# Convolution taps ordered behind each chain of queries or keys, and both ranges of rotated keys split in one operation per engine

## The chip, the core and the metric

The kernel runs on one core of one Trainium2 chip. The time is device microseconds of one execution; the kernel before takes 1058.18 us, the median of 3 runs. In this text TensorE is PE in the rows of the profile, VectorE is DVE, ScalarE is ACT, GpSimd is POOL and SyncE is SP.

## The reference

The network has two layers over 256 latent tokens (4 rows of 64 columns) and 256 context tokens, 1024 wide, in float32. Each layer has a token-mixing and a channel-mixing stage. The edited code belongs to the first of them: one input projection gives the columns of a convolution branch, of queries, keys and values of 8 heads, and of two gates.

```python
h = modulate(rmsnorm(x, norm1_g[l]), sh1, sc1)
p = h @ w_in[l]
q, k, v = (split_heads(u) for u in jnp.split(p[..., GLU_END:QKV_END], 3, axis=-1))
q = rope_2d(q, pos_row, pos_col)
k = rope_2d(k, pos_row, pos_col)
y_conv = conv_branch(p[..., :GLU_END], conv_dw[l], conv_dw_b[l], conv_ln_g[l],
                     conv_ln_b[l], w_conv_out[l])
y_attn = merge_heads(neighbourhood_attention(q, k, v, k_c, v_c, na_rpb[l])) @ w_na_out[l]
x = x + g1 * gated_merge(p[..., QKV_END:], y_conv, y_attn, w_out[l])
```

A latent query sees the keys of 16 columns in all 4 rows, with a bias, and all 256 context keys, in one softmax. In layer 0 the context tokens run through the same stage with an attention of their own; in layer 1, the last, they only give keys and values. The convolution branch is a gated linear unit, 31 taps along the tokens for each of its 512 channels, a LayerNorm, a silu and a projection.

## The kernel before

**Matmuls.** Tokens are columns, channels are partitions. A float32 product is made of three matmuls with reduced operands: every weight and every activation is kept as a high part and a remainder, and `mm3` (L197, L198, L199) adds high times high, remainder times high and high times remainder in PSUM. SyncE loads a block of weights (`raw`, 512 KB, four buffers), ACT rounds it to the high part (`whi`, L167 or L216), and the remainder comes from DVE (`wlo`, L168) or from ACT (L217) with an accumulating DMA of GpSimd (L218). Layer 0 works on 512 columns (latent and context tokens), layer 1 on 256, its keys on 512.

**PSUM.** There are 4 banks `main` for groups of the projection, and `sc` (2), `pt` and `po` for attention. A group has 24 matmuls per block of 128 channels. It can start only when the DVE and ACT operations that read its bank before have ended.

**Queries and keys.** `qk(j)` runs for the four pairs of heads j = 0 to 3. For queries and then for keys it calls `in_group` and sends DVE and ACT through a chain: product with the cosines (L859), swap of the halves (L860), product with the sines (L861), and their sum (L864 for queries, which also reorders columns into blocks; L869 for keys). Then high part and remainder of each piece of the result: ACT writes the high part (L881), DVE the remainder (L882). For keys the pieces are the context keys (`qk<-main`, 256 elements, read from PSUM) and two ranges of rotated columns, the last 40 of each row and the first 40 (`qk<-t`, 4 rows x 40, that is 160 elements). These are stored column by column, so that the four rows of a column lie side by side; neighbours of a row stand 16 bytes apart. For queries there is one latent piece of 256, and in layer 0 one of 256 for the context.

**Attention.** `att.pair` (on L884) queues the pair. Steps of attention are issued between groups of the projection: `products` (L495, TensorE), `scores` (bias and maximum on DVE, L516; exponential on ACT, L519; reciprocal on DVE, L521; scaling on ACT, L522), `turn` (transposes on TensorE, L561, and their copies on ACT, L564 or L567) and `values` (L578, L587; L595 and L596 take the result).

**Taps.** The convolution is 31 taps in each of 4 blocks, 124 in a layer: `tap` (L671 for the first of a block, L673 for the others), a multiply-add of a whole block on DVE. They wait in a list and are issued a few at a time by slots inside the groups of the projection (`rate`, 2 or 3 per slot). `conv_tap` issues a tap with an order behind the operation in `after[0]`: a tap that is issued later may not come ahead of it on DVE. Before, `after[0]` is set only by scores, latent (L516) and context (L530); the scheduler is free to put taps between the operations of a chain. A layer's taps end in `ss` (L949 to L951), the sum for the LayerNorm, for which TensorE waits at L955.

The order on each engine is fixed when the kernel is built; engines wait for one another through semaphores.

Of the kernel before, what the change touches and what calls it, by code (L numbers as in the profile page):

```python
# [8 lines left out]
F32 = mybir.dt.float32  # L9
# [3 lines left out]
ALU = mybir.AluOpType  # L13
# [7 lines left out]
GW = 64  # L21
# [11 lines left out]
LAT, CTX = slice(0, S), slice(S, 2 * S)  # L33
ROWS = S // GW
NB_, BC = 4, 16
WC, TC = 32, 40
BASE = (0, 8, 24, 32)
KL, KX, KN = ROWS * TC, ROWS * TC + S, 2 * ROWS * TC + S
# [15 lines left out]
def trunk(ctx: ExitStack, tc: tile.TileContext, xt, cvec, crow, wall, wada, params, bias_t, rope_t, out):  # L54
# [368 lines left out]
    class Attention:  # L423
# [147 lines left out]
        def values(self, what, js, pT, bank):  # L571
# [19 lines left out]
            for n, j in enumerate(js):  # L591
# [3 lines left out]
                act.copy(to[0], src)  # L595
                dve.tensor_tensor(to[1], src, to[0].bitcast(F32), ALU.subtract)  # L596

    def blocks(ap):
        return ap.rearrange("p (r b c) -> p b r c", r=ROWS, b=NB_)

# [31 lines left out]
    for l in range(DEPTH):  # L632
# [5 lines left out]
        with ExitStack() if last else start as e1a:  # L638
# [74 lines left out]
            with ExitStack() as e1b:  # L713
# [129 lines left out]
                def qk(j):  # L843
# [4 lines left out]
                    for what in range(2):  # L848
                        w = T if what == 0 else 2 * S
                        sc = HD ** -0.5 if what == 0 else 1.0  # L850
                        ps = in_group((T_Q, T_K)[what] + j, slice(0, w))
                        if what == 0:
                            with tc.issue_after(lastdma[0].ins):
                                sp.dma_start(bt, bias_t[l, j])
                        r1, r2 = tmp(), tmp()
                        got = back(ps[:, :w])
                        lat, ctx_ = (got[:, 0], got[:, 1]) if w > S else (got, None)
                        part = halves if w == S else lambda a: a
                        dve.tensor_tensor(part(r1[:, LAT]), lat, part(rope[:, 0, :]), ALU.mult)  # L859
                        dve.stream_shuffle(part(r2[:, LAT]), lat, SWAP16)  # L860
                        dve.tensor_tensor(r2[:, LAT], r2[:, LAT], rope[:, 1, :], ALU.mult)  # L861
                        if what == 0:
                            rq = tmp()
                            dve.tensor_tensor(  # L864
                                rq[:, LAT].rearrange("p (b r c) -> p b r c", b=NB_, r=ROWS),
                                blocks(r1[:, LAT]), blocks(r2[:, LAT]), ALU.add,
                            )
                        else:
                            dve.tensor_tensor(r1[:, LAT], r1[:, LAT], r2[:, LAT], ALU.add)  # L869
                        f = eb.tile([P, 2, KN if what else w], F32R, tag="qk"[what], bufs=2, name=nm("qk"))  # L870
                        if what == 0:
                            to = [([f[:, a, LAT] for a in range(2)], rq[:, LAT])]
                            if T > S:
                                to.append(([f[:, a, CTX] for a in range(2)], ctx_))
                        else:
                            rv_ = r1[:, LAT].rearrange("p (r c) -> p r c", r=ROWS)
                            to = [([f[:, a, KCTX] for a in range(2)], ctx_)]
                            for d, c in ((slice(0, KL), slice(GW - TC, GW)), (slice(KX, KN), slice(0, TC))):
                                to.append(([f[:, a, d].rearrange("p (c r) -> p r c", r=ROWS) for a in range(2)], rv_[:, :, c]))
                        for (hi, lo), src in to:  # L880
                            act.activation(hi, src, AF.Identity, scale=sc)  # L881
                            end = dve.scalar_tensor_tensor(lo, src, sc, hi.bitcast(F32), ALU.mult, ALU.subtract)  # L882
                        both.append(f)
                    att.pair(j, *both, bt, end)  # L884

# [471 lines left out]
```

## Time and profile before

| | |
|---|---|
| median of 3 runs | 1058.18 us |
| lowest and highest | 1057.49 and 1059.27 us |
| the profiled execution | 1054.58 us, its span 1052.8 us |
| mean granted clock of TensorE | 0.997 |
| instructions | 17991 |
| HBM read | 187.63 MB, 179 GB/s over the span with what is written |

The profiled execution is one of its own, 3.6 us below the median. The profile names an instruction by engine, line of the kernel, operation and tiles, output first (`qk<-t`); a duration runs from the start to the end of one instruction, and since neighbours overlap on an engine, two of them can start closer together than either lasts. Layer 0's token mixing takes from about 58 to 240 us, its channel mixing to about 685, layer 1's token mixing to about 840, and its channel mixing the rest.

### The profile page before, as it was taken

What the parts mean: (1) busy time and instruction counts of PE and PEld (TensorE: products, weight loads), DVE (VectorE), ACT (ScalarE), POOL (GpSimd) and SP (SyncE); (2) the same over time, 40 slices, a digit from 0 to 9 for tenths busy, and PEclk for the clock granted to TensorE, in tenths of its full rate; (3) what the DMA queues carried; (4) which work ended last, traced back from release to release, by engine and by line L of the source; (5) the groups of instructions that cost most, each with busy time, mean ns of one, the idle gap of its engine ahead of it and who ended that gap; (6) DMA issues with size and microseconds to landing.
All of it is one profiled execution on the core that took longest, in us unless ns stands there. A gap on an engine that the chain in (4) does not pass through costs nothing.

```text
span 1052.8 us, 17991 instructions
## 1 busy us (share of the span) xinstructions
PE 1032.4 (98%) x6886; PEld 932.9 (89%) x6886; DVE 893.2 (85%) x1608; ACT 565.6 (54%) x921; POOL 43.7 (4%) x59
## 2 busy tenths in 40 slices
PE   9999999999999999999999999999999999999997
PEld 7787788888889988888888889999889999999996
DVE  6568899999998787878788888799899988988883
ACT  4458768545434644444444223545777666766652
POOL 1111110011000000000000000000000000000000
PEclk9999999999999999999999999999999999999998
DMA  9989674888945345454545887556734485666781
GB/s 374 305 221 229 156 181 121 258 255 236 305 146 177 104 140 160 140 164 143 166 145 160 301 289 249 180 189 209 208 123 135 161 292 176 193 201 199 221 283 57
DMA packets 59511, 209.26 MB, mean 199 GB/s; under 512 B 7201, under 2 KB 7457, under 8 KB 59425
## 3 DMA queue, kind: packets, MB, share of 16 engines
q1 hardware_dynamic: 54384, 190.77, 55.3%
q0 software_dynamic: 4752, 17.30, 8.7%
q8 instruction: 54, 0.88, 0.3%
q14 instruction: 33, 0.26, 0.1%
q10 hardware_dynamic: 288, 0.04, 0.0%
HBM read 187.63 MB, written 1.05 MB: 179 GB/s over the span
## 4 chain that ended last, share of the span: by engine, by line
PE 68%; DVE 17%; ACT 5%; DMA 4%; issue 3%; SPq 1%; DVEq 0%; ACTq 0%
PE main L197 20%; PE main L198 20%; PE main L199 20%; DVE cb L673 6%; PE main L736 4%; DVE wlo L168 3%; DMA raw<-in_wall 2%; DVE t L304 2%; DMA own<-in_wada 1%; SPq L728 1%; PE sc L197 1%; PE sc L199 1%; PE sc L198 1%; DVE qk L882 1%; ACT pp L519 1%
## 5 line engine op out<-in xcount | busy, mean ns | idle before, releaser
L197 PE MATMUL main<-h,whi 128*128 128x256 f32 (+1 forms) x1328 | 433.1, 326 | 1.2 <-DVE qk L882 1.2
L198 PE MATMUL main<-h,whi 128*128 128x256 f32 (+1 forms) x1328 | 430.2, 324 | 0.9 <-DVE h L1001 0.7
L199 PE MATMUL main<-h,wlo 128*128 128x256 f32 (+1 forms) x1328 | 429.9, 324 | 1.2 <-DVE wlo L168 1.1
L167 ACT CAST whi<-raw 128x1024 fp32r<-128x1024 f32 (+1 forms) x211 | 218.3, 1039 | 234.8 <-PE main L198 173.6
L168 DVE TENSOR_TENSOR wlo<-raw,whi 128x1024 fp32r<-128x1024 f32 (+1 forms) x211 | 253.6, 1208 | 67.2 <-ACT whi L167 66.4
L197 PEld LDWEIGHTS main<-h,whi 128*128 128x128 f32 x1328 | 252.8, 190 | 22.0 <-issue 1.3
L199 PEld LDWEIGHTS main<-h,wlo 128*128 128x128 f32 x1328 | 252.5, 190 | 18.5 <-DVE wlo L168 1.8
L198 PEld LDWEIGHTS main<-h,whi 128*128 128x128 f32 x1328 | 252.7, 190 | 18.3 <-DVE h L1001 1.0
L304 DVE CUSTOM_DVE_ANT_0 t<-own,sb,par 128x1024 bf16<-128x1024 f32 x120 | 151.8, 1282 | 6.8 <-DMA own<-in_wada 6.8
L673 DVE SCALAR_TENSOR_TENSOR cb<-u,par,cb 128x512 f32<-128x512 f32 (+1 forms) x240 | 144.7, 620 | 2.8
L198 PE MATMUL main<-fl,whi 128*128 128x256 f32 (+1 forms) x396 | 122.8, 310 | 0.0
L197 PE MATMUL main<-fh,whi 128*128 128x256 f32 (+1 forms) x396 | 122.8, 310 | 0.0
L199 PE MATMUL main<-fh,wlo 128*128 128x256 f32 (+1 forms) x396 | 122.5, 310 | 0.0
L197 PEld LDWEIGHTS main<-fh,whi 128*128 128x128 f32 x396 | 75.6, 191 | 3.8 <-ACT fh L1095 0.2
L198 PEld LDWEIGHTS main<-fl,whi 128*128 128x128 f32 x396 | 75.6, 191 | 3.7 <-DVE fl L1096 0.2
L199 PEld LDWEIGHTS main<-fh,wlo 128*128 128x128 f32 x396 | 75.5, 191 | 3.6
L216 ACT CAST whi<-raw 128x1024 fp32r<-128x1024 f32 x33 | 34.6, 1049 | 36.0 <-PE main L198 30.5
L404 ACT ACTIVATE h<-t,mod 128x256 fp32r<-128x256 f32 x56 | 25.2, 503 | 34.8 <-DVE t L403 34.3
L218 POOL DMA_DIRECT2D wlo<-raw x33 | 28.9, 877 | 258.9 <-ACT wlo L217 107.6
L736 PE MATMUL main<-whi,h 128*128 128x512 f32 x128 | 38.5, 386 | 0.2
L1105 ACT ACTIVATE t<-t 128x512 f32<-128x512 f32 x22 | 13.9, 632 | 41.3 <-DVE t L1074 41.3
L217 ACT ACTIVATE wlo<-whi 128x1024 fp32r<-128x1024 f32 x33 | 35.0, 1061 | 0.5
(214 smaller groups left out, 1268.8 us busy)
## 6 DMA issues: line engine op xcount, KB each, us to landing
raw<-in_wall SPq DMA_DIRECT2D x240, 512.0 KB, 4.3
own<-in_wada SPq DMA_DIRECT2D x72, 512.0 KB, 4.7
wlo<-raw POOLq DMA_DIRECT2D x33, 512.0 KB, 5.4
raw<-in_wada SPq DMA_DIRECT2D x16, 512.0 KB, 5.8
bias<-in_bias_t SPq DMA_DIRECT2D x8, 520.0 KB, 5.3
row<-in_wada SPq DMA_DIRECT2D x8, 512.0 KB, 5.1
sb<-in_crow SPq DMA_DIRECT2D x5, 512.0 KB, 4.8
x<-in_xt SPq DMA_DIRECT2D x4, 512.0 KB, 5.1
```

What stands on the lines that cost most here:

```text
L167: act.copy(hi[:, c], r[:, c])
L168: dve.tensor_tensor(lo[:, c], r[:, c], hi[:, c].bitcast(F32), ALU.subtract)
L197: pe.matmul(ps, w[0], order(xh), start=start, stop=False)
L198: pe.matmul(ps, w[0], order(xl), start=False, stop=False)
L199: pe.matmul(ps, w[1], order(xh), start=False, stop=stop)
L216: act.copy(hi, r)
L217: act.mul(lo, hi.bitcast(F32), -1.0)
L218: pool.dma_start(lo, r, accum_op=ALU.add)
L304: dve.tensor_tensor_reduce(tmp().bitcast(BF16), r, v, 1.0, pr(l, BADA + n, 1), ALU.mult, ALU.add, mods[l][:, n, s : s + 1])
L404: high = act.activation(hi[:, c], y[:, c], AF.Identity, bias=b)
L673: dve.scalar_tensor_tensor(cb[j], src, w, cb[j], ALU.mult, ALU.add)
L736: mm = pe.matmul(pv[t], h1[n == 1][k][:, c], runs(w[n == 2][:, b]), start=k + n == 0, stop=k == KD - 1 and n == 2)
```

## The change

Two things are changed in `qk(j)`. First, the loop over the two ranges of keys is gone: a helper `steps` builds one access pattern over both ranges, and one ACT copy and one DVE subtraction of 2 x 4 x 40 = 320 elements take the place of two and two. Second, `after[0] = end` is set behind the chain of queries and behind that of keys, so that taps issued from then on are ordered behind its last operation on DVE (L888 for keys, L883 for queries), as they are behind scores.

```diff
@@ -594,6 +594,10 @@
                 src = po[:, c].rearrange("p (b r c) -> p b r c", b=NB_, r=ROWS) if what == LAT else po[:, c]
                 act.copy(to[0], src)
                 dve.tensor_tensor(to[1], src, to[0].bitcast(F32), ALU.subtract)
+
+    def steps(a, first, *dims):
+
+        return bass.AP(tensor=a.tensor, offset=a.offset + first, ap=[a.ap[0], *dims])
 
     def blocks(ap):
         return ap.rearrange("p (r b c) -> p b r c", r=ROWS, b=NB_)
@@ -873,13 +877,16 @@
                             if T > S:
                                 to.append(([f[:, a, CTX] for a in range(2)], ctx_))
                         else:
-                            rv_ = r1[:, LAT].rearrange("p (r c) -> p r c", r=ROWS)
                             to = [([f[:, a, KCTX] for a in range(2)], ctx_)]
-                            for d, c in ((slice(0, KL), slice(GW - TC, GW)), (slice(KX, KN), slice(0, TC))):
-                                to.append(([f[:, a, d].rearrange("p (c r) -> p r c", r=ROWS) for a in range(2)], rv_[:, :, c]))
                         for (hi, lo), src in to:
                             act.activation(hi, src, AF.Identity, scale=sc)
                             end = dve.scalar_tensor_tensor(lo, src, sc, hi.bitcast(F32), ALU.mult, ALU.subtract)
+                        if what:
+                            hi, lo = (steps(f[:, a], 0, (KX, 2), (1, ROWS), (ROWS, TC)) for a in range(2))
+                            src = steps(r1, GW - TC, (TC - GW, 2), (GW, ROWS), (1, TC))
+                            act.copy(hi, src)
+                            end = dve.tensor_tensor(lo, src, hi.bitcast(F32), ALU.subtract)
+                        after[0] = end
                         both.append(f)
                     att.pair(j, *both, bt, end)
```

The lines behind the helper are numbered 4 higher in the changed kernel, and by 6 or 7 more behind the edit: L859, L860, L861, L864 and L869 become L863, L864, L865, L868 and L873, L881 and L882 become L882 and L883, L887 and L888 are new, L671 and L673 become L675 and L677, and the gate's L711 becomes L715. TensorE's and GpSimd's rows stay in their order; on SyncE the load of a bias and one of weights change places. DVE and ACT have 8 instructions fewer each.

DVE in layer 0, the chain of keys of pair 1 (`main_943`, TensorE's group) up to the first scores of the same pair (`sc`). Before:

```order
L859 TENSOR_TENSOR t_1012<-main_943,rope_196 128x256
L860 STREAM_SHUFFLE t_1013<-main_943 128x256
L673 SCALAR_TENSOR_TENSOR cb_0_184<-u_0_197,par,cb_0_184 128x512
L861 TENSOR_TENSOR t_1013<-t_1013,rope_196 128x256
L882 SCALAR_TENSOR_TENSOR qk_1018<-main_943,qk_1018 128x256
L869 TENSOR_TENSOR t_1012<-t_1012,t_1013 128x256
L673 SCALAR_TENSOR_TENSOR cb_0_184<-u_0_197,par,cb_0_184 128x512 x2
L882 SCALAR_TENSOR_TENSOR qk_1018<-t_1012,qk_1018 128x4x40 x2
L673 SCALAR_TENSOR_TENSOR cb_0_184<-u_0_197,par,cb_0_184 128x512 x3
L516 ISA sc_1063,mx_1079<-sc_1063,bias_893 128x2x208
```

With the change, from the same group (now `main_941`):

```order
L863 TENSOR_TENSOR t_1010<-main_941,rope_196 128x256
L677 SCALAR_TENSOR_TENSOR cb_0_184<-u_0_197,par,cb_0_184 128x512
L864 STREAM_SHUFFLE t_1011<-main_941 128x256
L865 TENSOR_TENSOR t_1011<-t_1011,rope_196 128x256
L873 TENSOR_TENSOR t_1010<-t_1010,t_1011 128x256
L883 SCALAR_TENSOR_TENSOR qk_1016<-main_941,qk_1016 128x256
L888 TENSOR_TENSOR qk_1016<-t_1010,qk_1016 128x2x4x40
L677 SCALAR_TENSOR_TENSOR cb_0_184<-u_0_197,par,cb_0_184 128x512 x5
L516 ISA sc_1059,mx_1075<-sc_1059,bias_891 128x2x208
L516 ISA mx_1075 128x1
L677 SCALAR_TENSOR_TENSOR cb_0_184<-u_0_197,par,cb_0_184 128x512
```

The taps that stood between L869 and L882 have moved behind L888, and one of them stands between the two scores.

DVE in layer 1, behind the last scores of pair 0 (`L516` on `main_7303` and `main_7293`, just ahead of these rows), with the end of the chain of keys of pair 1 (`qk_7348`, `qk_7338`) and the start of the chain of queries of pair 2 (`main_7392`, `main_7380`). Before:

```order
L673 SCALAR_TENSOR_TENSOR cb_1_6567<-u_1_6580,par,cb_1_6567 128x256
L671 TENSOR_SCALAR cb_2_6568<-u_2_6581,par 128x256
L673 SCALAR_TENSOR_TENSOR cb_1_6567<-u_1_6580,par,cb_1_6567 128x256
L521 RECIPROCAL ri_7331<-sm_7329 128x1
L673 SCALAR_TENSOR_TENSOR cb_2_6568<-u_2_6581,par,cb_2_6568 128x256
L673 SCALAR_TENSOR_TENSOR cb_1_6567<-u_1_6580,par,cb_1_6567 128x256
L521 RECIPROCAL ri_7339<-sm_7337 128x1
L673 SCALAR_TENSOR_TENSOR cb_2_6568<-u_2_6581,par,cb_2_6568 128x256
L882 SCALAR_TENSOR_TENSOR qk_7348<-t_7342,qk_7348 128x4x40
L673 SCALAR_TENSOR_TENSOR cb_1_6567<-u_1_6580,par,cb_1_6567 128x256
L859 TENSOR_TENSOR t_7428<-main_7392,rope_6578 128x256
L882 SCALAR_TENSOR_TENSOR qk_7348<-t_7342,qk_7348 128x4x40
```

With the change:

```order
L521 RECIPROCAL ri_7321<-sm_7319 128x1
L521 RECIPROCAL ri_7329<-sm_7327 128x1
L863 TENSOR_TENSOR t_7416<-main_7380,rope_6570 128x256
L864 STREAM_SHUFFLE t_7417<-main_7380 128x256
L888 TENSOR_TENSOR qk_7338<-t_7332,qk_7338 128x2x4x40
L677 SCALAR_TENSOR_TENSOR cb_1_6559<-u_1_6572,par,cb_1_6559 128x256
L675 TENSOR_SCALAR cb_2_6560<-u_2_6573,par 128x256
L677 SCALAR_TENSOR_TENSOR cb_1_6559<-u_1_6572,par,cb_1_6559 128x256
L865 TENSOR_TENSOR t_7417<-t_7417,rope_6570 128x256
L677 SCALAR_TENSOR_TENSOR cb_1_6559<-u_1_6572,par,cb_1_6559 128x256
L868 TENSOR_TENSOR t_7421<-t_7416,t_7417 128x256
```

The taps that stood around the two reciprocals and between the two L882 now stand behind L888, and L888 behind both reciprocals and the first two operations on the next queries.

ACT at the same place. Before:

```order
L519 ACTIVATE pp_7336,sm_7337<-main_7303,mx_7334 128x416
L522 ACTIVATE pp_7328<-pp_7328,ri_7331 128x416
L881 ACTIVATE qk_7348<-t_7342 128x4x40
L522 ACTIVATE pp_7336<-pp_7336,ri_7339 128x416
L881 ACTIVATE qk_7348<-t_7342 128x4x40
L711 ACTIVATE g_1_7389<-main_7355 128x256
```

With the change:

```order
L519 ACTIVATE pp_7326,sm_7327<-main_7293,mx_7324 128x416
L522 ACTIVATE pp_7318<-pp_7318,ri_7321 128x416
L522 ACTIVATE pp_7326<-pp_7326,ri_7329 128x416
L887 CAST qk_7338<-t_7332 128x2x4x40
L715 ACTIVATE g_1_7377<-main_7343 128x256
```

The high parts of the two ranges stood on either side of the last L522; the one L887 stands behind it.

ACT in layer 1 one pair later, at the end of the exponentials of pair 1 (`pp_7550` and `pp_7538`) with the high parts of the keys of pair 2 (`qk_7562`, `qk_7550`). Before:

```order
L519 ACTIVATE pp_7542,sm_7543<-pt_7516,mx_7540 128x416
L519 ACTIVATE pp_7550,sm_7551<-main_7517,mx_7548 128x416
L522 ACTIVATE pp_7542<-pp_7542,ri_7545 128x416
L522 ACTIVATE pp_7550<-pp_7550,ri_7553 128x416
L881 ACTIVATE qk_7562<-t_7556 128x4x40 x2
L711 ACTIVATE g_2_7604<-main_7569 128x256
L167 CAST whi_7836<-raw_7835 128x1024
```

With the change:

```order
L522 ACTIVATE pp_7522<-pp_7522,ri_7525 128x416
L522 ACTIVATE pp_7530<-pp_7530,ri_7533 128x416
L519 ACTIVATE pp_7538,sm_7539<-main_7505,mx_7536 128x416
L882 ACTIVATE qk_7550<-main_7426 128x256
L715 ACTIVATE g_2_7590<-main_7555 128x256
L522 ACTIVATE pp_7538<-pp_7538,ri_7541 128x416
L167 CAST whi_7820<-raw_7819 128x1024
L887 CAST qk_7550<-t_7544 128x2x4x40
```

The high part of the context keys (`qk<-main`), which stood ahead of all exponentials of this softmax, now stands behind the last of them, and that of the ranges behind one more L522 and a weight cast (L167).

## The prediction

> **What bounds the kernel now.** I read the page's busy shares first, then the table of stretches, then what TensorE waits for, then the groups by shape, and last the timeline around single chains.
>
> ```profile
> PE 1032.4 (98%) x6886; PEld 932.9 (89%) x6886; DVE 893.2 (85%) x1608; ACT 565.6 (54%) x921; POOL 43.7 (4%) x59
> ...
> 105.00:145.00 40.00, 37.99 (x258) 32.29 (x257) 35.98 (x78) 30.18 (x66) 5.21 (x6) 1.00 0.66 160
> 740.00:800.00 60.00, 58.63 (x555) 52.77 (x554) 57.07 (x148) 47.63 (x103) 3.17 (x3) 1.00 0.51 154
> 800.00:840.00 40.00, 38.83 (x352) 37.82 (x350) 38.00 (x85) 24.34 (x48) 0.71 (x1) 1.00 0.51 159
> ```
>
> After the length of a stretch stand the busy times of PE, PEld, DVE, ACT and POOL, then the granted clock. TensorE is busy for 98% of the span, so another order on DVE can win no more than the gaps it leaves TensorE. The edited code runs from 58 us on (layer 0) and around 740 to 800 us (layer 1). In layer 1 DVE is nearly full as well: 57.07 of 60 us, then 38.00 of 40. A hole made in its row there is not easily filled later. The clock is 1.00 in all three, so it is no term. What TensorE waits for over the whole span (total us, times, longest):
>
> ```profile
> PE pt L370 <- DVE ss L356: 2.0, 3, 1.0
> ...
> PE sc L495 <- ACT pT L567: 1.7, 1, 1.7
> PE main L197 <- DVE qk L882: 1.2, 2, 0.6
> ...
> PE po L955 <- DVE ss L951: 1.0, 1, 1.0
> PE sc L495 <- ACT qk L881: 0.9, 1, 0.9
> ...
> PE sc L495 <- DVE qk L882: 0.6, 1, 0.6
> ```
>
> Two things are to be seen. The waits that earlier chains can end (L881, L882, and L567, whose copies stand behind chain operations on ACT) add up to 0.9 + 1.2 + 0.6 + 1.7 = 4.4 us, 0.4% of the time: about the ceiling of the gain. And each stage ends in a wait on DVE itself: layer 0 in `ss L951` (1.0 us), layer 1 in `ss L356` (1.0 us the longest). Behind such a wait only DVE's own finishing time counts, and what TensorE gained earlier is lost there unless DVE comes earlier too. **So I make the sum on DVE's time, layer by layer.**
>
> **The merge.** Per chain of keys two operations of 160 elements become one of 320, on ACT and on DVE; eight chains in all, so 8 instructions fewer on each engine.
>
> ```profile
> L881 ACT ACTIVATE qk<-t 128x160 fp32r<-128x160 f32 x8 | 4.4, 620 | 1.1 <-DVE t L869 1.1
> L882 DVE SCALAR_TENSOR_TENSOR qk<-t,qk 128x160 fp32r<-128x160 f32 x8 | 4.3, 561 | 0.3
> L521 DVE RECIPROCAL ri<-sm 128x1 f32<-128x1 f32 x16 | 2.6, 160 | 1.5 <-ACT pp L519 1.5
> ...
> L882 DVE SCALAR_TENSOR_TENSOR qk<-t,qk 128x256 fp32r<-128x256 f32 x4 | 1.7, 423 | 0.5 <-ACT qk L881 0.5
> ```
>
> 160 elements take 561 ns in layer 1, more than the 423 ns of 256 that lie side by side. No row has the 320-element form. Durations overlap, so I count from start to start: the pair below at 763.90 gives way to a tap at 764.83, 0.93 us for 320 elements; the pair at 96.20 in layer 0 gives way at 96.91, 0.71 us. Bounds for the merged operation are 0.4 us (somewhat over the 256-element form, as L869, 256 elements, gives way to a tap 0.33 us after its start, from 94.41 to 94.74 below) and 0.93 (nothing saved). I take 0.65, nearest to the layer 0 pair less one start: 0.06 us saved per chain in layer 0, 0.28 in layer 1; on ACT I take 0.5 to 0.65. If the bounds held instead, the eight chains would differ by about 1 us to either side; I keep that for the range.
>
> [...]
>
> **Layer 0: later taps, earlier chains.** DVE, TensorE and ACT around the keys of pair 1 (its scores at 99.16) and the context softmax behind pair 2 (start, duration, operation, idle time before it; between them the group of DVE's first score operations in layer 0, with its idle time):
>
> ```profile
> 94.41 0.42 DVE L869 TENSOR_TENSOR t<-t,t 128x256 f32<-128x256 f32 x1
> 94.74 1.54 DVE L673 SCALAR_TENSOR_TENSOR cb<-u,par,cb 128x512 f32<-128x512 f32 x2
> 96.20 0.81 DVE L882 SCALAR_TENSOR_TENSOR qk<-t,qk 128x160 fp32r<-128x160 f32 x2
> 96.91 2.33 DVE L673 SCALAR_TENSOR_TENSOR cb<-u,par,cb 128x512 f32<-128x512 f32 x3
> 99.16 0.59 DVE L516 CUSTOM_DVE_ANT_0 sc<-sc,bias 128x416 f32<-128x416 f32 x1
> ...
> 96.04 0.44 PE L495 MATMUL sc<-qk,qk 64*128 64x416 f32 x2 [0.87 <-ACT qk L881]
> 97.07 0.62 PE L495 MATMUL sc<-qk,qk 64*128 64x416 f32 x4 [0.58 <-DVE qk L882]
> ...
> L516 DVE CUSTOM_DVE_ANT_0 sc<-sc,bias 128x416 f32<-128x416 f32 x4 | 2.4, 592 | 3.3 <-PE sc L495 3.3
> ...
> 125.32 0.81 ACT L881 ACTIVATE qk<-t 128x160 fp32r<-128x160 f32 x2 [1.58 <-DVE t L869]
> 127.98 1.05 ACT L567 COPY pT<-sc 128x512 f32<-128x512 f32 x2
> ...
> 128.60 1.11 PE L495 MATMUL sc<-qk,qk 64*128 64x416 f32 x5 [1.69 <-ACT pT L567]
> ```
>
> The two taps between L869 and L882 (1.46 us from 94.74 to 96.20) now stand behind L888. L888 must then wait for ACT's L887, some 0.45 us, so pair 1's chain ends about 1 us earlier, and TensorE gets back 1.0 to 1.2 of its 0.87 + 0.58. The scores, however, have the same taps ahead of them as before, one more even ahead of the second L516: five, a score, a sixth, a score. With the holes of about 0.65 us in the chain of queries and 0.45 at L888, where taps ran before, the softmax comes 0.7 to 1.1 us later, and the transposes take back what the products won. For pair 2 one tap fewer stands ahead and ACT's two operations become one, so L567, for which TensorE waits at 128.60, comes some 0.8 us earlier (0.73 of a tap and 0.1). On DVE's time: holes +1.1, merges 4 × −0.06, and of the 3.3 us that DVE waits for products in front of the scores about 1.2 (0.8 for pair 2, half of that for the others): **−0.4 us at `ss L951`** (1.1 − 0.24 − 1.2). The ends are −2.4 (1.2 + 0.8 + 0.4 kept) and +1.1 (holes only).
>
> **Layer 1, pair 1: a hole behind the scores.** From here taps may not start before L888, and both reciprocals, L863, L864 and L888 stand ahead of them. The softmax of the pair before, as it ran:
>
> ```profile
> 746.08 0.14 DVE L516 DVE_READ_ACCUMULATOR2_ANT mx<- 128x1 f32 x1
> 746.08 0.48 DVE L673 SCALAR_TENSOR_TENSOR cb<-u,par,cb 128x256 f32<-128x256 f32 x1
> ...
> 746.86 0.20 ACT L519 ACTIVATION_READ_ACCUMULATOR pp<-pt,mx 128x1 f32 x1
> 747.44 0.21 ACT L519 ACTIVATION_READ_ACCUMULATOR pp<-main,mx 128x1 f32 x1
> 747.53 0.65 ACT L522 ACTIVATE pp<-pp,ri 128x416 f32<-128x416 f32 x1
> 748.07 0.64 ACT L881 ACTIVATE qk<-t 128x160 fp32r<-128x160 f32 x1
> 748.39 0.66 ACT L522 ACTIVATE pp<-pp,ri 128x416 f32<-128x416 f32 x1
> ...
> 753.85 0.82 PE L495 MATMUL sc<-qk,qk 64*128 64x416 f32 x3 [0.19 <-ACT pT L564]
> ```
>
> DVE is free at 746.22 (746.08 + 0.14). Before, taps started at once. Now the first reciprocal waits for ACT until 747.06, the second until 747.65; L863 and L864 (0.33 each) then run to 748.45. ACT does both L522 from 747.53, 0.54 apart, so its L887 starts at about 748.6 and lets L888 start at about 749.25. In those 3.03 us DVE works 0.2 (two reciprocals, less than their 160 ns each from start to start) + 0.67, so **2.2 us stand empty** where taps and one of the two L881 and L882 ran. Next to the hole the chain of queries of pair 2 comes 0.7 us earlier, which ends the wait for L564 that TensorE has at 753.85.
>
> **Layer 1, pair 2: the bank and a second hole.**
>
> ```profile
> 761.09 0.42 DVE L882 SCALAR_TENSOR_TENSOR qk<-main,qk 128x256 fp32r<-128x256 f32 x1
> ...
> 761.65 0.45 PE L197 MATMUL main<-h,whi 128*128 128x512 f32 x1 [0.55 <-DVE qk L882]
> ...
> 762.20 1.18 ACT L522 ACTIVATE pp<-pp,ri 128x416 f32<-128x416 f32 x2
> 763.27 1.04 ACT L881 ACTIVATE qk<-t 128x160 fp32r<-128x160 f32 x2
> 763.90 1.04 DVE L882 SCALAR_TENSOR_TENSOR qk<-t,qk 128x160 fp32r<-128x160 f32 x2
> 764.83 0.46 DVE L673 SCALAR_TENSOR_TENSOR cb<-u,par,cb 128x256 f32<-128x256 f32 x1
> ```
>
> TensorE's next group waited for L882 to free its bank. Its successor L883 now needs an ACT copy that stands behind the last exponential, and itself stands behind that exponential's reciprocal and a weight split. ACT is done with the last exponential at about 762.2, as before; the copy takes it to 762.55, DVE's reciprocal and L865 meanwhile to 762.65, L883 to 763.0, where L882 ended at 761.5: that group starts 1.5 us later. ACT then has the gate (0.45), one L522 (0.54), a weight cast (1.0) and L887 (0.6), to about 765.15, while DVE has L873, L863 and L864, 1.0 us from 763.0 on. Before L888 another **1.2 us stand empty**. Pair 3 has a split as cover and loses some 0.15. In sum 2.2 + 1.2 + 0.15 − 3 × 0.28 = **+2.7 us on DVE**. It has to reach `L356`:
>
> ```profile
> 821.51 0.42 DVE L356 TENSOR_TENSOR ss<-ss,t 128x256 f32<-128x256 f32 x1
> ```
>
> TensorE already waited 1.0 us for this row, and DVE has 38.00 busy of the 40 us around it, so nothing ahead of it takes up 2.7. The ends are −0.5 (ACT early enough, 0.28 saved three times) and +3.8 (holes, nothing saved). Queues past which something moves: SyncE swaps one bias load with one weight load, cost nothing while weights have the 0.51 DMA share above; GpSimd's and TensorE's rows stay as they were.
>
> **The sum**: −0.4 + 2.7 = +2.3 us. On the profiled execution's 1054.58 that is 1056.9; the median of the runs is 1058.18, 3.6 above it, and I predict **1060.5** there.
>
> **Rivals.**
> - *Chains win* (faster): the gains stay in both layers and the holes are refilled. For it: the 4.4 us of waits are real. Against it: both stages end in DVE waits. It gives −1.2 − 0.8 − 0.4 in layer 0 and −0.2 − 1.2 (both bank waits) in layer 1: −3.8, 1054.4. Chance 0.20.
> - *Covered* (no change): the order moves, but DVE's holes replace waits it has anyway, and gains and losses cancel. TensorE's row order is unchanged, which speaks for it; 57.07 of 60 us speaks against. 1058.2. Chance 0.17.
> - *Holes in both layers* (slower): the holes in layer 0, +1.1, also reach `ss L951` with nothing shortened, and layer 1 loses 3.2 (the 3.55 of its holes with under half of the merge's gain). It decides as soon as L888 waits in both layers for an ACT copy that stands behind another's work. 1058.2 + 4.3 = 1062.5. Chance 0.13.
>
> **How the numbers follow.** My forecast has the remaining 0.50, with a range of its own from 1058.8 to 1062.0 (layer 1's hole by ±1.0, the merge by ±0.5). A measurement of this kernel tells 0.2%, 2.1 us, from no change; the forecast lies at that edge and gives about half to each side. Faster: 0.20. Same: 0.17 + 0.23 = 0.40. Slower: 0.13 + 0.27 = 0.40. The range 1055.0 to 1062.4 leaves out about half of the faster rival and half of the slowest, under 2 in 10.
>
> **What would show it.** Right: in layer 1, DVE idle time of about 2 us in front of two reciprocals and L888 in pair 1, about 1 us in pair 2; a longer TensorE wait for L883; `L356` about 2.5 us later against the start of the stage, with a wait of over 1 us still on it; in layer 0 the waits at L495 for L887 and L888 mostly gone, with the wait at L561 for L522 grown. Wrong: no wait left on `L951` or `L356`, or an L888 of 0.4 us.

## The result, and the profile after

The changed kernel takes **1063.93 us** (median of 6 runs, 1061.42 to 1065.77) against 1057.84 (6 runs, 1055.06 to 1059.76): a ratio of **1.0057, 95% interval 1.0037 to 1.0077**. It is slower by 6.1 us, where the forecast said 2.3 and the range ended at 1062.4. The profiled execution took 1062.81 us, its span is 1061.0 (before 1052.8).

The stretches of the changed kernel and what its TensorE waits for, in the columns used before:

```profile
58.00:105.00 47.00, 45.15 (x231) 37.94 (x230) 38.74 (x84) 30.86 (x52) 7.14 (x9) 0.96 0.89 224
105.00:145.00 40.00, 36.94 (x262) 30.70 (x261) 34.98 (x74) 30.15 (x68) 4.35 (x5) 0.96 0.56 149
...
740.00:800.00 60.00, 55.69 (x490) 50.01 (x490) 55.42 (x146) 40.92 (x86) 4.72 (x4) 1.00 0.51 157
```

```profile
PE sc L495 <- ACT pT L567: 2.1, 1, 2.1
PE main L197 <- ACT pp L519: 2.0, 1, 2.0
...
PE pt L370 <- DVE ss L356: 1.8, 3, 1.0
PE main L197 <- DVE qk L883: 1.6, 1, 1.6
PE sc L495 <- ACT qk L887: 1.5, 1, 1.5
PE po L578 <- DVE ol L596: 1.4, 1, 1.4
...
PE sc L495 <- DVE qk L888: 0.4, 1, 0.4
...
PE po L962 <- DVE ss L958: 0.3, 1, 0.3
```

None of the waits that the earlier chains could end has gone: L567 has 2.1 us (before 1.7), the first scores 1.5 + 0.4 (before 0.9 + 0.6), and the bank waits have grown from 1.2 to 2.0 + 1.6. The granted clock, 1.00 before, is 0.96 in two stretches.

Where the loss arises is seen by setting TensorE's rows of both profiles side by side, since their order is the same. Against before, TensorE is late by

| at (time in before) | changed | changed again | order only | order, layer 0 | order, layer 1 | merge only |
|---|---|---|---|---|---|---|
| 213 us, end of layer 0's taps | +4.07 | +4.88 | +2.56 | +3.10 | +1.48 | +4.09 |
| 742 us, ahead of layer 1's pair 1 | +4.15 | +5.73 | +3.15 | +4.33 | +3.50 | +5.45 |
| 821 us, end of layer 1's taps | +8.31 | +10.44 | +8.12 | +4.32 | +8.13 | +5.82 |
| **from 742 to 821** | **+4.16** | **+4.71** | **+4.97** | −0.01 | **+4.63** | +0.37 |

The other columns belong to kernels of the next section. Layer 1 is clear: 4.2 to 5.0 us with the new order, next to nothing without. Layer 0 is not: "order, layer 1" runs layer 0 as before and is 1.48 late there, so one profile is uncertain by some 1.5 us at that place; and "merge only", without the new order, is 4.09 late there, though its times are only 0.15% longer. For the whole, the times decide.

### The profile page after: what moved, and what is told of

It is laid out like the page before. It is cut to its first block, busy times and chain, and to the rows that moved or that the text cites. A ratio compares the mean times of both kernels' runs of the same rounds, so it can differ in the third digit from the quotient of the medians.

```text
span 1061.0 us, 17970 instructions
## 1 busy us (share of the span) xinstructions
PE 1034.8 (98%) x6886; PEld 934.1 (88%) x6886; DVE 898.1 (85%) x1600; ACT 566.0 (53%) x913; POOL 44.8 (4%) x59
## 4 chain that ended last, share of the span: by engine, by line
PE 69%; DVE 18%; ACT 5%; DMA 4%; issue 3%; SPq 1%; DVEq 0%; ACTq 0%; POOLq 0%
PE main L197 20%; PE main L198 20%; PE main L199 20%; DVE cb L677 7%; PE main L740 4%; DVE wlo L168 3%; DMA raw<-in_wall 2%; DVE t L304 1%; SPq L732 1%; PE sc L197 1%; PE sc L199 1%; PE sc L198 1%; ACT pp L519 1%; DMA wlo<-raw 1%; PE po L230 1%
## 5 line engine op out<-in xcount | busy, mean ns | idle before, releaser
L167 ACT CAST whi<-raw 128x1024 fp32r<-128x1024 f32 (+1 forms) x211 | 218.6, 1040 | 229.9 <-PE main L198 170.0
L198 PEld LDWEIGHTS main<-h,whi 128*128 128x128 f32 x1328 | 253.1, 191 | 18.4 <-DVE h L1008 1.0
L677 DVE SCALAR_TENSOR_TENSOR cb<-u,par,cb 128x512 f32<-128x512 f32 (+1 forms) x240 | 147.0, 616 | 4.4
L216 ACT CAST whi<-raw 128x1024 fp32r<-128x1024 f32 x33 | 34.6, 1048 | 42.5 <-PE main L198 34.5
L1112 ACT ACTIVATE t<-t 128x512 f32<-128x512 f32 x22 | 13.9, 632 | 41.0 <-DVE t L1081 41.0
L217 ACT ACTIVATE wlo<-whi 128x1024 fp32r<-128x1024 f32 x33 | 34.9, 1059 | 0.5
```

The lines of the kernel that those rows point to most:

```text
L167: act.copy(hi[:, c], r[:, c])
L198: pe.matmul(ps, w[0], order(xl), start=False, stop=False)
L216: act.copy(hi, r)
L217: act.mul(lo, hi.bitcast(F32), -1.0)
L677: dve.scalar_tensor_tensor(cb[j], src, w, cb[j], ALU.mult, ALU.add)
```

## The experiments

Each ratio is to the kernel before, run beside it, with its 95% interval; 0.1% is 1.06 us.

**One part alone.** `order_only` is the kernel before with the taps' new order; `merge_only` is the changed kernel without it.

```diff
+                        after[0] = end
                         both.append(f)
```

> The order of taps alone: ranges of keys split one by one as before, with taps ordered behind each chain. Theory A (two causes: holes on DVE in layer 1 come from the order, 3.5 us; in layer 0 the loss comes from L887 waiting for L883, which only the merge brings): layer 1 loses 3.5 to 4.2 us as in the changed kernel, layer 0 within 1 us of before, in all +3 to +5 us, 1061 to 1063. Rival B (the merge is what costs, order is free): within 1 us of before. Rival C (the order costs in both layers): as the changed kernel, +6 us.

1.0080 [1.0061, 1.0099], 1064.37 us, nearest to rival C.

> The merge alone: one operation per engine for both ranges, taps free as before. Theory A: L887 still waits for L883 on the context keys, but taps stand between and cover DVE, so DVE has no hole over 0.3 us; products in layer 0 wait up to 1 us longer; -1 to +1.5 us in all. Rival B (the merge costs): +3 us or more, with TensorE's waits at L495 as in the changed kernel.

1.0015 [1.0001, 1.0029], 1057.94 us. The order is the loss. The merge, which I had put at a gain of 1.1 us, gains nothing.

**Without the wait inside the merge.** One access pattern over both ranges also spans the context keys between them, and in the changed kernel ACT's L887 waits 0.87 us for DVE's L883, which reads those; the row is in the section on layer 0, the 1.50 us that the scores wait for L887 under *The clock*. Here ACT makes both high parts before DVE makes either remainder.

```diff
                         for (hi, lo), src in to:
                             act.activation(hi, src, AF.Identity, scale=sc)
+                        if what:
+                            h2, l2 = (steps(f[:, a], 0, (KX, 2), (1, ROWS), (ROWS, TC)) for a in range(2))
...
+                            act.copy(h2, s2)
+                        for (hi, lo), src in to:
                             end = dve.scalar_tensor_tensor(lo, src, sc, hi.bitcast(F32), ALU.mult, ALU.subtract)
```

> Both parts, but ACT writes the high parts of context keys and of both ranges ahead of either remainder, so that the high part of the ranges need not wait for the remainder of the context keys (L883 in the changed kernel). Theory A: in layer 0 the chains of keys end 0.4 to 1 us earlier, TensorE's two waits fall below 1.9 us in all and its clock stays at full speed there, so layer 0 gets back some 3 to 4 us; layer 1 keeps its holes: 1061 to 1062.5. Rival C (order alone): 1063 to 1065, the clock falls as before.

1.0101 [1.0080, 1.0122].

> The merge without that wait and without the order of taps. Theory A: the best of the four, 0 to 2 us under before, 1056 to 1058. Rival B (one operation of 320 elements ends the chain later than two that overlap between ACT and DVE): +0.5 to +2 us.

1.0030 [1.0015, 1.0045]. ACT's and DVE's rows of `both_no_false_wait` for pair 1 in layer 0 (start, duration, operation, idle time before it):

```profile
95.31 0.76 ACT L886 CAST qk<-t 128x320 fp32r<-128x320 f32 x1 [0.59 <-DVE t L873]
```

```profile
96.10 0.42 DVE L888 SCALAR_TENSOR_TENSOR qk<-main,qk 128x256 fp32r<-128x256 f32 x1 [0.88 <-ACT qk L886]
96.56 0.74 DVE L890 TENSOR_TENSOR qk<-t,qk 128x320 fp32r<-128x320 f32 x1
```

ACT's copy now waits only for the sum L873 that it reads, but DVE's first remainder waits 0.88 us in its turn. The wait has moved, not gone, and the time is, if anything, worse (1.0101 against 1.0057 and 1.0067 for the changed kernel); the runs do not show why.

**Which layer, which chain.** The line `after[0] = end` under a condition:

```diff
+                        if l == 0:
+                            after[0] = end
```

(and with `l == 1`, `what == 0` for queries, `what == 1` for keys).

> The order of taps alone, in layer 0 only. The run with the order in both layers ended layer 0 2.6 us late and lost 5.8 more behind it. Theory D (the losses are separate and add up): +1.5 to +3.5 us. Rival E (layer 0's loss is made up by later waits on TensorE, layer 1 carries everything): within 1 us of before.

1.0021 [1.0009, 1.0033].

> The order of taps alone, in layer 1 only. Theory D: +4 to +6 us, DVE with some 3.5 us of holes ahead of L521 and L882 of pairs 1 and 2, TensorE's wait at L882's bank 2 us longer. Rival E: the whole +8 us.

1.0051 [1.0034, 1.0067]. Together 0.72%, near the 0.80% of both: layer 0 costs some 2.2 us, layer 1 some 5.4.

> Order only behind the chains of queries, both layers. Theory F (the hole comes from the last operation of the keys, which waits for an ACT operation behind the softmax of the pair before): 0 to +2.5 us, no hole over 0.5 us in front of L882 in layer 1. Rival G (any order behind a chain costs alike): about half of the +8 us.

1.0033 [1.0018, 1.0048].

> Order only behind the chains of keys, both layers. Theory F: most of the loss, +5 to +8 us, with the holes of 2 and 1 us ahead of L882 in pairs 1 and 2 of layer 1. Rival G: about half, +4 us.

1.0039 [1.0023, 1.0056]. The queries, which have no merge and no wait over ranges, cost about as much as the keys. That is rival G, not theory F.

**The clock.** Rows of TensorE in the changed kernel at pair 1's scores and behind them, and the same place in a second profile of the same code:

```profile
96.51 0.44 PE L495 MATMUL sc<-qk,qk 64*128 64x416 f32 x2 [1.50 <-ACT qk L887]
97.31 0.62 PE L495 MATMUL sc<-qk,qk 64*128 64x416 f32 x4 [0.35 <-DVE qk L888]
...
99.70 0.63 PE L199 MATMUL main<-h,wlo 128*128 128x512 f32 x1
100.13 0.63 PE L197 MATMUL main<-h,whi 128*128 128x512 f32 x1
```

```profile
96.45 0.44 PE L495 MATMUL sc<-qk,qk 64*128 64x416 f32 x2 [1.40 <-ACT qk L887]
97.25 0.62 PE L495 MATMUL sc<-qk,qk 64*128 64x416 f32 x4 [0.36 <-DVE qk L888]
...
98.65 0.38 PE L198 MATMUL main<-h,whi 128*128 128x512 f32 x1
98.86 0.38 PE L199 MATMUL main<-h,wlo 128*128 128x512 f32 x1
```

In the first, matmuls start 0.43 us apart, at half the rate of the second (0.21), and the granted clock is 0.50 from 98.0 to 101.4 us. The same profile has it at 0.50 once more, from 132.2 to 135.5 us, behind the wait of 2.13 us that ends at 131.44. The suspicion was that the 1.50 + 0.35 us of waiting ahead of them lets the clock down; the "about 2 us" of theory H is an estimate, and the same profile also has a wait of 1.97 us with a clock of 1.00 behind it (last section). `filled_wait` puts seven matmuls of the unit matrix (14 in the profile's count), whose result is overwritten, in front of pair 1's products.

```diff
+                if self.l == 0 and j == 1 and not qt:
+                    for _ in range(7):
+                        pe.matmul(sl(out[0], 0), ident, ident, start=True, stop=True)
                 self.product([ps[:, :NS_] for ps in out], q, k, slice(qt * P, (qt + 1) * P), d)
```

> The changed kernel as it is, beside the two others on the same chip: 1.003 to 1.008 of before, clock 0.992 to 0.995.

1.0067 [1.0051, 1.0084]; the loss repeats.

> The changed kernel with seven matmuls of a unit matrix, into a bank that the products overwrite, ahead of pair 1's products in layer 0, where TensorE waits 1.5 us for L887. Theory H (TensorE's clock halves after it has stood for about 2 us within a few): no half-speed matmuls behind that wait, mean clock 0.001 to 0.002 higher, 1 to 2 us faster than the changed kernel. Rival I (the clock falls whatever TensorE does there): the same time and clock, or slower by the matmuls.

1.0077 [1.0060, 1.0093]. TensorE's rows of `filled_wait`:

```profile
94.64 1.72 PE L503 MATMUL sc<-ident 128*128 128x128 f32 x14
96.29 0.44 PE L495 MATMUL sc<-qk,qk 64*128 64x416 f32 x2
96.99 0.62 PE L495 MATMUL sc<-qk,qk 64*128 64x416 f32 x4 [0.25 <-DVE qk L891]
```

The wait is filled and the matmuls behind it run at full rate (0.21 us apart), but the time is no better. In the same profile a stretch some ten us later has a lower clock instead (0.66 granted from 107 to 112 us), behind waits of 0.48, 0.38, 1.30 and 0.37 us. The second profile of the changed kernel had no half rate behind pair 1's scores either, and its transposes were late by 2.33 us all the same (2.39 in the first): there the clock only fills a wait for the softmax. Nor does the loss need the clock: the profiled execution of `order_only`, with a granted clock of 0.998 (before 0.997), took 1062.88 us against 1054.58.

**Where taps may start, and how many run first.** `order_behind_sum` lets taps start behind the sum (L864 or L869) instead of the last remainder. `scores_first` goes the other way: from the kernel before, layer 0 issues no tap between queueing a pair and its scores.

```diff
...
+                        after[0] = added
                         both.append(f)
```

```diff
+            self.hold = self.l == 0
...
-                    while due >= 1:
+                    while due >= 1 and not att.hold:
```

> No merge; taps ordered behind L864 or L869, the sum of the rotated products, and not behind the last operation of the chain, so that they may fill DVE's wait for ACT. Theory J (in layer 1 it is the holes in front of L521 and L882 that cost): holes in pairs 1 and 2 together under 1.5 us instead of 3, layer 1 loses at most 2 us, in all +2 to +4.5 us. Rival K (the banks that TensorE waits for cost, not the holes): +6 us or more.

1.0023 [1.0011, 1.0034]: under a third of `order_only`'s loss is left. In all it came out as theory J said; layer 1, though, loses 3.1 us in its profile, not at most 2.

> The kernel before, with no tap issued in layer 0 from the end of a chain of keys until that pair's products and scores are issued, so that 8, 24, 48 and 72 taps stand ahead of the four scores instead of 16, 30, 54 and 78. Layer 1 as before. Theory L (in layer 0 the softmax, and the transposes and copies behind it, are set by the taps ahead of the scores, which the change leaves as many as they were): the scores come 1 to 4 us earlier and the waits at L561 for L522, and at L495 for L564, go: 0.5 to 2 us faster than before. Rival M (the taps only come back later, and TensorE waits for L951 instead): within 1 us of before, or up to 2 us slower.

1.0088 [1.0073, 1.0104]. With 8, 24, 48 and 72 taps ahead of the scores of the four pairs, not 16, 30, 54 and 78, DVE stood idle 27.5 us up to the end of layer 0's taps instead of 16.1. Taps ahead of the scores are cover here, not delay: the kernel is 9.3 us slower, which neither theory had. And their number is the same in before and in the changed kernel, but for one at pair 1 (30 and 29), so it cannot be the difference.

**Neighbours on DVE.** The last theory came from the DVE rows themselves (next section): an operation that reads what the one right ahead of it wrote starts later (0.46 to 0.48 us behind it for 256 elements) than another would (0.34). The alternating kernels take taps from two blocks in turn, so that a tap seldom follows one of its own block.

```diff
+            def next_tap():
+                i = next((n for n, (j, _) in enumerate(taps) if j != block[0]), 0)
+                block[0] = taps[i][0]
+                conv_tap(*taps.pop(i))
...
-                            conv_tap(*taps.pop(0))
+                            next_tap()
```

> The kernel before, with each tap taken from another block of channels than the last one, where two are waiting. The traces so far show a tap that follows one of its own block 0.79 us after its start (512 columns) or 0.52 (256), and one that follows anything else 0.66 or 0.39 to 0.40: 0.125 us more. The count of such neighbours falls from 79 to 14. Theory N (this price is real, and DVE's time decides both token-mixing stages): DVE saves up to 8 us, TensorE loses its waits at L951 and L356 and part of those at L495 and L882: 1 to 4 us faster than before. Rival O (DVE's time does not decide): within 1 us.

1.0020 [1.0003, 1.0037], 1058.36 us.

> The changed kernel with the same alternation: neighbours of one block fall from 124 to 20, 13 us of DVE. Theory N: most of the loss goes, the time is -1 to +3 us of before. Rival P (the holes in front of L521 and L888 and the later softmax cost, not the neighbours): +5 to +7 us as the changed kernel.

1.0070 [1.0044, 1.0095], 1064.27 us. Neither kernel gains, and the most that theory N left of the loss, 3 us, is passed: the change still costs 0.50%. What the traces show stands in the next section.

**The copies of pair 2.** `copies_first` orders one weight cast (L216, L217) behind the copies of L567 for which TensorE waits at 128.60, in the kernel before, in the changed one, and in the kernel before with alternating taps.

```diff
-        act.copy(hi, r)
...
+        with tc.issue_after(held.ins) if held else ExitStack():
+            act.copy(hi, r)
...
+                hold.extend([self.copied] * 4)
```

> The kernel before, with one weight's two ACT operations (L216, L217, some 2.0 us) ordered behind the copies of the context transposes (L567) in layer 0, for which TensorE waits 1.7 us at 128.6. Theory Q (that wait sits at the edge of the clock's halving: with it 1.7 to 2.3 us long the traces show half speed behind it or not): the wait falls under 0.5 us, no half speed there in any profile, 1 to 3 us faster than before, mean clock 0.001 to 0.002 higher. Rival R (the softmax behind it sets the pace all the same): within 1 us of before.

1.0000 [0.9985, 1.0015], 1056.56 us.

> The changed kernel with the same order of those copies. Theory Q: the wait of 2.1 us at 131.4 and the half speed behind it go, 2 to 4 us faster than the changed kernel, 1.003 to 1.005 of before. Rival R: as the changed kernel, 1.006 to 1.007.

1.0082 [1.0069, 1.0095].

> The kernel before with that order of copies and taps taken from two blocks in turn. If both DVE's dependent neighbours and this wait cost, 2 to 5 us faster than before; if alternation gains nothing, as the first of these three.

0.9998 [0.9979, 1.0016], 1055.25 us. TensorE's row of `copies_first_before`, 1.60 us earlier than before and without a wait:

```profile
127.00 1.02 PE L502 MATMUL sc<-qk,qk 64*128 64x416 f32 x6
```

At the next softmax (155 us) 0.21 of it is left, and at 213 us nothing. So rival R held in the kernel before, and theory Q in neither. No kernel here is measurably faster than before.

## Why the prediction was wrong, step by step

**The view was right.** The sum was made on DVE's time. In layer 0 the last row of DVE that TensorE waits for came 4.07 us later, as TensorE did, with 0.3 us of the wait of 1.0 left; in layer 1 `L356` moved from 821.51 to 829.82,

```profile
829.82 0.42 DVE L356 TENSOR_TENSOR ss<-ss,t 128x256 f32<-128x256 f32 x1
```

that is 8.31 later, of which 4.15 came from ahead of the stage's pair 1, with the wait of 1.0 us on it as before. What failed is the sum made on it, in layer 0 in its sign and in layer 1 in its size.

**The step that failed: layer 0, "−0.4 us at `ss L951`" (1.1 − 0.24 − 1.2).** By the times layer 0 loses 2.2 us (1.0 to 3.5, `order_layer0`). I counted holes, merges and shorter waits, and took moved operations at their old price, which put the spacing of neighbours on DVE at nothing without a reason; and I credited 1.2 us for a wait that came back elsewhere. DVE's rows of the changed kernel for pair 1, and ACT's L887 among them:

```profile
93.96 0.45 DVE L864 STREAM_SHUFFLE t<-main 128x256 f32<-128x256 f32 x1
94.44 0.42 DVE L865 TENSOR_TENSOR t<-t,rope 128x256 f32<-128x256 f32 x1
94.90 0.42 DVE L873 TENSOR_TENSOR t<-t,t 128x256 f32<-128x256 f32 x1
95.24 0.42 DVE L883 SCALAR_TENSOR_TENSOR qk<-main,qk 128x256 fp32r<-128x256 f32 x1
96.49 0.76 DVE L888 TENSOR_TENSOR qk<-t,qk 128x320 fp32r<-128x320 f32 x1 [0.83 <-ACT qk L887]
97.15 3.90 DVE L677 SCALAR_TENSOR_TENSOR cb<-u,par,cb 128x512 f32<-128x512 f32 x5
100.96 0.59 DVE L516 CUSTOM_DVE_ANT_0 sc<-sc,bias 128x416 f32<-128x416 f32 x1
```

```profile
95.69 0.76 ACT L887 CAST qk<-t 128x320 fp32r<-128x320 f32 x1 [0.87 <-DVE qk L883]
```

L865 reads L864's output and starts 0.48 us behind it; L873 reads L865's and starts 0.46 behind; but L883, which does not read L873's, starts 0.34 behind it. Each lasts 0.42 to 0.45 us: the ones that read their neighbour start just after its end, L883 before it. In the same chain of before, an operation or a tap stands between any two of which one reads the other, and nearly every step is 0.33 or 0.34:

```profile
93.74 0.42 DVE L861 TENSOR_TENSOR t<-t,rope 128x256 f32<-128x256 f32 x1
94.08 0.42 DVE L882 SCALAR_TENSOR_TENSOR qk<-main,qk 128x256 fp32r<-128x256 f32 x1
94.41 0.42 DVE L869 TENSOR_TENSOR t<-t,t 128x256 f32<-128x256 f32 x1
```

The five taps of the changed kernel are all of one block and take 3.81 us to the scores: four of 0.79, and 0.66 for the last, which no tap follows. This price stood in the rows of the prediction, where three taps take 2.25 us (96.91 to 99.16). The same place in `alternating_changed`, where the taps are of two blocks in turn:

```profile
96.09 4.07 DVE L683 SCALAR_TENSOR_TENSOR cb<-u,par,cb 128x512 f32<-128x512 f32 x6
100.07 0.60 DVE L516 CUSTOM_DVE_ANT_0 sc<-sc,bias 128x416 f32<-128x416 f32 x1
```

Six taps in 3.98 us, 0.66 each. In these rows a neighbour that depends on the one ahead costs some 0.12 us more (0.46 against 0.34, 0.79 against 0.66). The new order makes such pairs: a chain that runs unbroken reads itself, and the taps behind it come in one run.

To price them I took every DVE row from 58 us to the end of layer 0's taps, and from 690 us (in before) to the row of L356 above; the distance from its start to the next start, less the short distance usual for its form in before (the tenth percentile), was put down as a wait where the next row starts over 0.06 us after its end, and else to spacing. The levels of spacing hang on which forms are pooled (with others they come out at about half); the differences between kernels move by some 0.5 us only, and these are what is read.

| layer 0 / layer 1, us | span | waits | spacing |
|---|---|---|---|
| before | 153.7 / 130.8 | 16.3 / 4.9 | 13.9 / 14.5 |
| changed | 157.9 / 135.1 | 16.8 / 6.9 | **17.8 / 17.3** |
| changed again | 158.7 / 135.1 | 17.7 / 6.2 | **17.7 / 17.7** |
| order only | 156.3 / 135.5 | 15.3 / 5.6 | **17.6 / 18.4** |
| order, layer 0 | 156.7 / 131.2 | 15.8 / 5.2 | **17.5** / 14.5 |
| order, layer 1 | 155.1 / 135.2 | 17.6 / 5.5 | 14.1 / **18.2** |
| merge only | 157.7 / 131.3 | 20.6 / 6.1 | 13.7 / 14.2 |
| order behind sum | 155.4 / 133.5 | 14.5 / 2.6 | **17.6 / 19.5** |
| alternating, before | 155.3 / 131.3 | 22.1 / 9.6 | 9.8 / 10.2 |
| alternating, changed | 154.6 / 134.8 | 19.6 / 13.0 | 11.8 / 10.6 |

Wherever the new order stands in a layer, with taps in their old sequence, spacing is 2.8 to 5.0 us larger, and where it doesn't, it is as before (13.7 to 14.5). Pairs of dependent neighbours are 73 instead of 48 in layer 0 and 62 instead of 37 in layer 1. In layer 0 the working is then +0.5 waits, +3.9 spacing and −0.2 merges, 4.2 us in this profile; the forecast had no such term. The times give the layer only 2.2 us, so the sum is not yet a price: the spacing is shown in DVE's rows, what it is worth in time is not (last paragraph of this section).

**Layer 0, the waits.** I let DVE's 3.3 us in front of the scores shrink by 1.2 and allowed 1.1 for holes. DVE's groups in layer 0 after the change:

```profile
L888 DVE TENSOR_TENSOR qk<-t,qk 128x320 fp32r<-128x320 f32 x4 | 3.4, 839 | 3.7 <-ACT qk L887 3.7
...
L516 DVE CUSTOM_DVE_ANT_0 sc<-sc,bias 128x416 f32<-128x416 f32 x4 | 2.4, 593 | 0.0
...
L883 DVE SCALAR_TENSOR_TENSOR qk<-t,qk 128x256 fp32r<-128x256 f32 x4 | 1.7, 422 | 0.7 <-ACT qk L882 0.5
```

All 3.3 are gone, and 3.7 + 0.7 stand in front of L888 and L883 in their place: I had worked out the holes for pair 1 only, and there without L887's wait for L883 (ACT stands idle 0.87 before it, above). So pair 1's chain, which I had end 1 us earlier, gave way at 97.15, before at 96.91, and TensorE got nothing back. The softmax came later, as expected, but by 1.8 us (from 99.16 to 100.96), not 0.7 to 1.1; and pair 2's L567, forecast 0.8 earlier, came 2.8 later. ACT was 1.9 late there already (its copy of the context keys starts at 125.22, before at 123.35), and L887, which waited for L883 again, added the rest:

```profile
128.18 0.79 ACT L887 CAST qk<-t 128x320 fp32r<-128x320 f32 x1 [2.58 <-DVE qk L883]
...
130.82 1.05 ACT L567 COPY pT<-sc 128x512 f32<-128x512 f32 x2
```

The rival *Holes in both layers* had the right sign and place here, with holes for its reason; net of the waits that went, they were only 0.5 us of the 4.2.

**Layer 1: the mechanism was right, its sum too small.** DVE's rows of the changed kernel behind the scores of pair 0, and L888 of pairs 2 and 3:

```profile
752.34 0.17 DVE L521 RECIPROCAL ri<-sm 128x1 f32<-128x1 f32 x1 [0.75 <-ACT pp L519]
752.93 0.17 DVE L521 RECIPROCAL ri<-sm 128x1 f32<-128x1 f32 x1 [0.42 <-ACT pp L519]
...
754.67 0.91 DVE L888 TENSOR_TENSOR qk<-t,qk 128x320 fp32r<-128x320 f32 x1 [0.88 <-ACT qk L887]
```

```profile
770.74 1.05 DVE L888 TENSOR_TENSOR qk<-t,qk 128x320 fp32r<-128x320 f32 x1 [1.09 <-ACT qk L887]
```

```profile
785.56 0.98 DVE L888 TENSOR_TENSOR qk<-t,qk 128x320 fp32r<-128x320 f32 x1 [0.35 <-ACT qk L887]
```

The holes are 2.05, 1.09 and 0.35 us where 2.2, 1.2 and 0.15 were forecast: 3.49 for 3.55, at the places named. Other waits shrank, so that the layer's waits grew by 2.0. Spacing, which the forecast lacked, grew by 2.8, and the operations themselves fell by 0.5: 4.3 us instead of 2.7. By the times layer 1 loses 5.4 us (3.6 to 7.1, `order_layer1`), twice the forecast, so 1.1 us more than this sum has; the interval covers both. Either part shows alone on DVE's row: `order_behind_sum` has fewer waits than before and still ends the layer 2.7 later; in the alternating kernels spacing differs by 0.4 only, and the change costs 3.5, nearly all of it waits. TensorE paid its 4.16 us at the banks (1.4, where 1.5 had been forecast, and 0.7), at `po` (1.4), and ahead of them at pair 1's products (0.6):

```profile
767.81 0.48 PE L197 MATMUL main<-h,whi 128*128 128x512 f32 x1 [1.97 <-ACT pp L519]
```

```profile
784.00 0.38 PE L197 MATMUL main<-h,whi 128*128 128x256 f32 x1 [1.56 <-DVE qk L883]
```

```profile
811.18 1.08 PE L578 MATMUL po<-pT,V 128*64 128x256 f32 x8 [1.42 <-DVE ol L596]
```

The bank that I had L883 free was freed by the last exponential (L519); L883 freed the next one, 16 us later. Of the signs named in advance, those of layer 1 were there (about 2 us and 1 us idle, the longer wait for L883, `L356` late with its wait still on it, but by 4.2 us and not 2.5); in layer 0 the wait at L561 grew as named (0.3 to 0.6 us), but the waits at L495 did not go.

**The merge.** In layer 0 L888 gives way 0.66 us after its start (96.49 to 97.15), the 0.65 assumed; for pairs 2 and 3 it is 0.68 and 0.69, but 0.93 for pair 0. In layer 1 it is 0.79, 0.93 and 0.81 for pairs 1 to 3: a saving of 0.09 us against the pair's 0.93, not 0.28. The lower bound of 0.4 never occurred. 0.93 less the 0.06 that I took for one start should have been the price in layer 1.

**"The clock is 1.00 in all three, so it is no term."** True of that profile, wrong as a conclusion: over 11 runs the changed kernel's mean granted clock is 0.9938, over 104 of before 0.9954, and among the runs of before beside the experiments 0.001 goes with 0.84 us (among the changed kernel's 11 with 0.16). By the first, some 1.3 us of the loss go with the clock, an estimate. Whether it is their cause was not settled: at the one place tried, filling the wait left the time as it was, and `order_only` lost its 8 us in a profile without a lower clock.

**What stays open.** What spacing alone is worth in time was not isolated. Most of the loss goes with the holes: `order_behind_sum`, with all of the spacing but 3.8 us fewer waits than `order_only`, loses 0.23% instead of 0.80%. Alternating taps took the layer 0 loss away in the trace (154.6 us with the change, 155.3 without); the times cannot tell, since layer 0 is 0.21% of the time, and the change costs 0.50% with alternation and 0.57% or 0.67% without, each known to 0.2 or 0.3% only. What is left with alternation, 5.3 us, is as much as layer 1 alone costs, which would fit that spacing is the loss of layer 0 and the holes that of layer 1; it is not shown. Nor do the two alternating profiles show it: against alternating without the change, TensorE loses 3.7 us from 742 to 821 us and 2.4 between 213 and 300, but with the change its matmuls of 512 columns stand 0.43 us apart, at half rate, from 770.57 to 776.28 and again near 296, and the granted clock of that profile is 0.988. In the kernel before, alternating lowers spacing by 4 us per layer, and waits take up all of it: spacing saved is not yet time saved.

## What to carry to other kernels

On an engine that is nearly full, an order that runs a chain "without interruption" also puts each operation behind the one that it reads: price the spacing of the new neighbours from rows (here 0.46 against 0.34 us for 256 elements, 0.79 against 0.66 for a tap), not the operations alone. The rows give what the engine's time grows by; how much of it the kernel's time feels hangs on the waits around it. The work that stood between was cover for two things, for that spacing and for the other engine's turn, and both come due when it is moved behind the chain (here 3.9 and 2.8 us of spacing in the two layers, 0.5 and 2.0 us of waits). A wait ended early is worth only what the next wait leaves of it: 1.6 us won at pair 2 by `copies_first_before` were gone one softmax later.

## What the runs showed of the hardware that was not expected

- **A dependent neighbour on DVE cost some 0.12 us** in the changed kernel and in before: 0.46 to 0.48 us from start to start for 256 elements instead of 0.33 to 0.34, 0.79 for a tap of 512 elements behind one of its own block instead of 0.66. In pair 1's chain it starts 0.03 and 0.04 us after the end of the one that it reads (L865, L873), where L883, which doesn't read its neighbour, starts 0.08 us before that neighbour's end.
- **Matmuls at half rate behind short waits, but not behind all.** 0.43 us apart instead of 0.21 behind waits of 1.50 + 0.35 us in one profile; behind 1.40 + 0.36 in another of the same code, none. In the first the granted clock is 0.50 again behind 2.13 us, but stays at 1.00 behind 1.97 and 1.56 us in layer 1 (764 to 790 us); in before it stays at 1.00 behind 1.69 us (128 to 136 us). No length of wait parts the two, and what lets the clock down was not shown.
- **The copy over two ranges waited for the operation on what lies between them**: 0.87 us of L887 for L883, which touches neither range, in the changed kernel. In `both_no_false_wait`, where the copy is issued ahead of that remainder, this wait is gone: the copy stands 0.59 us for the sum L873 that it reads.
